# A decoder layer on eight cores: attention over the last 384 keys with a test, contiguous halves of the sequence, and pairs of tiles kept on chip

## The chip, the cores and the metric

The kernel runs on the eight cores of one Trainium2 chip as one program. The time of a run is the device time of its slowest core, in microseconds (us). Executions fall in a fast and a slow state (the kernel before took 8993 and 9005 us in its two fast runs, 9149 to 9858 in the others). The engines are PE (matmul; PEld is its weight load), DVE (VectorE), ACT (ScalarE), POOL (GpSimd) and SP, which here only issues DMAs.

## The reference, cut to what matters

```python
# x: (4, 8192, 1024) float32; 8 heads of 128; D_FF = 2816
h = x + 0.5 * swiglu(rms_norm(x), w_in1, w_out1)             # w_in: 1024 x 5632, w_out: 2816 x 1024
u = rms_norm(h)
c_b, c_c, c_x, q, k, v, g_conv, g_attn = split(u @ w_mix_in)  # 1024 x 8192
y_conv = (c_b * causal_conv3(c_c * c_x)) @ w_conv_out
# stick-breaking attention, strictly causal, z = q.k / sqrt(128):
#   a[t, s] = sigmoid(z[t, s]) * prod over s < j < t of (1 - sigmoid(z[t, j]))
y_attn = (a @ v) @ w_attn_out
h = h + (sigmoid(g_conv) * y_conv + sigmoid(g_attn) * y_attn) @ w_mix_out
h = h + 0.5 * swiglu(rms_norm(h), w_in2, w_out2)
h = h + sigmoid(rms_norm(h) @ w_ple_gate) * (p @ w_ple_proj)
return rms_norm(h)
```

The weight of a key is a product over all keys between it and the query. With factors of about one half it vanishes within some hundred keys.

## The kernel before

Two cores share a sequence. Each owns every other block of 512 tokens. In a first stage it runs the first feed-forward and the q, k, v projections, with k and v for all 8192 tokens, since attention needs them; k, q, v and the residual go to HBM. In a second stage it runs attention, and weaves everything else (`c_iter`) in, a few matmuls at a time.

```python
for i in range(NO):                              # 8 chunks of 1024 tokens, 512 of them its own
    dma(SP, xtb.dsem, xt[:], xsrc[:, :, t0:t0 + 1024], writes=[xtb])
    rmsnorm(...); ffn(..., 1024); rmsnorm(...)   # then q (512 tokens), k and v (1024 tokens)
...
top = (2 * i + 1) * 4
for gk in range(top + 3, -1, -1):                # every key tile back to token 0
    ...
# for each tile and head: scores (PE), Exp (ACT), Ln (ACT), two triangular matmuls that sum
# the logarithms over keys (PE), Exp (ACT), product (DVE), times v (PE)
...
c_advance(i)                                     # a few steps of c_iter between attention steps

def g_gate(tt, ttb, pg, pgb):                    # a sigmoid of Exp, +1 and a reciprocal
    op(ACT, lambda: nc.scalar.activation(out=tt[:], in_=pg[:], func=AF.Exp, scale=-1.0), ...)
    op(DVE, lambda: nc.vector.tensor_scalar(..., scalar1=1.0, op0=ALU.add), ...)
    op(DVE, lambda: nc.vector.reciprocal(out=tt[:], in_=tt[:]), ...)
```

At the start all weights are cast from float32 to bf16, from HBM to HBM; later they are streamed through a ring in SBUF. ACT loads its tables 18 times in the profiled run, 1283 ns each, never at these gates (L510). (Cuts are marked with dots.)

Of the kernel before, what the change touches and what calls it, by code (L numbers as in the profile page):

```python
# [9 lines left out]
BF16 = mybir.dt.bfloat16  # L10
AF = mybir.ActivationFunctionType
ALU = mybir.AluOpType

D = 1024
# [6 lines left out]
NEGBIG = -30000.0  # L21
RING = 3
SLOT_ELEMS = 4096

class Buf:
    __slots__ = ("name", "w", "r", "dsem")

    def __init__(self, name):
        self.name = name
        self.w = None  # L30
        self.r = {}
        self.dsem = None

class DSem:
    __slots__ = ("sem", "cnt")

    def __init__(self, sem):
        self.sem = sem
        self.cnt = 0

class Eng:
# [7 lines left out]
    def wait(self, ev):  # L49
        sem, val = ev  # L50
        if sem is self.sem and not self.selfwait:
            return
        if self.waited.get(sem, 0) >= val:
            return
        self.h.wait_ge(sem, val)
        self.waited[sem] = val

def _deps(reads, writes):
    deps = {}
    for b in reads:  # L60
        if b.w is not None:
            s, v = b.w
            if deps.get(s, 0) < v:
                deps[s] = v
    for b in writes:
        if b.w is not None:
            s, v = b.w
            if deps.get(s, 0) < v:
                deps[s] = v
        for s, v in b.r.items():  # L70
            if deps.get(s, 0) < v:
                deps[s] = v
    return deps

def _record(ev, reads, writes):
    s, v = ev
    for b in reads:
        if b.r.get(s, 0) < v:
            b.r[s] = v
    for b in writes:  # L80
        b.w = ev
        b.r = {}

def op(eng, fn, reads=(), writes=()):
    for s, v in _deps(reads, writes).items():
        eng.wait((s, v))
    ins = fn()
    ins.then_inc(eng.sem, 1)
    eng.cnt += 1
    ev = (eng.sem, eng.cnt)  # L90
    _record(ev, reads, writes)
    return ev

def op_group(eng, fns, reads=(), writes=()):
    for s, v in _deps(reads, writes).items():
        eng.wait((s, v))
    ins = None
    for fn in fns:
        ins = fn()
    ins.then_inc(eng.sem, 1)  # L100
    eng.cnt += 1
    ev = (eng.sem, eng.cnt)
    _record(ev, reads, writes)
    return ev

def dma(q, ds, out_ap, in_ap, reads=(), writes=(), extra=()):
    deps = _deps(reads, writes)
    for s_, v_ in extra:
        if deps.get(s_, 0) < v_:
            deps[s_] = v_  # L110
    if ds.cnt:
        if deps.get(ds.sem, 0) < ds.cnt:
            deps[ds.sem] = ds.cnt
    for s, v in deps.items():
        q.wait((s, v))
    q.h.dma_start(out=out_ap, in_=in_ap).then_inc(ds.sem, 16)
    ds.cnt += 16
    ev = (ds.sem, ds.cnt)
    _record(ev, reads, writes)
    return ev  # L120

def build(S):
    NCH = S // 512
    NO = NCH // 2
    NB = S // 128
    SO = S // 2
    nc = bass.Bass("TRN2", target_bir_lowering=False)

    def din(name, shape, dt=F32):
        return nc.dram_tensor(name, list(shape), dt, kind="ExternalInput").ap()  # L130

    xT = din("xT", [D, S])
    pT = din("pT", [PLE, SO])
    W = {
        "in1": din("w_in1", [D, 2 * DFF]),
        "out1": din("w_out1", [DFF, D]),
        "mix": din("w_mix", [D, 8 * D]),
        "co": din("w_co", [D, D]),
        "ao": din("w_ao", [D, D]),
        "mo": din("w_mo", [D, D]),  # L140
        "in2": din("w_in2", [D, 2 * DFF]),
        "out2": din("w_out2", [DFF, D]),
        "pg": din("w_pg", [D, D]),
        "pp": din("w_pp", [PLE, D]),
    }
    vecs_d = din("vecs", [128, 64])
    consts_d = din("consts", [128, 640])
    outT = nc.dram_tensor("outT", [D, SO], F32, kind="ExternalOutput").ap()

    kT_s = nc.dram_tensor("kT_s", [H, 128, S], BF16).ap()  # L150
    qT_s = nc.dram_tensor("qT_s", [H, 128, SO], BF16).ap()
    v_s = nc.dram_tensor("v_s", [128, NB, D], BF16).ap()
    h1_s = nc.dram_tensor("h1_s", [128, KC, SO], F32).ap()
    oT_s = nc.dram_tensor("oT_s", [128, H, SO], BF16).ap()

    slabs = {}

    def add_slabs(prefix, w_ap, col0, ncols, cw, nm):
        K = w_ap.shape[0]
        kc = K // 128  # L160
        ns = ncols // cw
        wb = nc.dram_tensor("wb_" + nm, [ns, 128, kc, cw], BF16).ap()
        src = w_ap.rearrange("(k p) n -> p k n", p=128)
        for j in range(ns):
            slabs[(prefix, j)] = (src[:, :, col0 + j * cw: col0 + (j + 1) * cw], wb[j], kc, cw)

    add_slabs("in1g", W["in1"], 0, DFF, 256, "in1g")
    add_slabs("in1u", W["in1"], DFF, DFF, 256, "in1u")
    add_slabs("out1", W["out1"], 0, D, 128, "out1")
    add_slabs("mix", W["mix"], 0, 8 * D, 512, "mix")  # L170
    add_slabs("co", W["co"], 0, D, 512, "co")
    add_slabs("ao", W["ao"], 0, D, 512, "ao")
    add_slabs("mo", W["mo"], 0, D, 512, "mo")
    add_slabs("in2g", W["in2"], 0, DFF, 256, "in2g")
    add_slabs("in2u", W["in2"], DFF, DFF, 256, "in2u")
    add_slabs("out2", W["out2"], 0, D, 128, "out2")
    add_slabs("pg", W["pg"], 0, D, 512, "pg")
    add_slabs("pp", W["pp"], 0, D, 1024, "pp")

    plan = []  # L180
    for i in range(NO):
        for j in range(11):
            plan += [("in1g", j), ("in1u", j)]
        plan += [("out1", dt) for dt in range(8)]
        plan += [("mix", s) for s in (6, 7, 8, 9, 10, 11)]
    for i in range(NO):
        plan += [("mix", 2), ("mix", 4), ("mix", 3), ("mix", 5)]
        plan += [("mix", 0), ("mix", 1)]
        plan += [("mix", 12), ("co", 0), ("mix", 13), ("co", 1)]
        plan += [("mix", 14), ("ao", 0), ("mix", 15), ("ao", 1)]  # L190
        plan += [("mo", 0), ("mo", 1)]
        for j in range(11):
            plan += [("in2g", j), ("in2u", j)]
        plan += [("out2", dt) for dt in range(8)]
        plan += [("pp", 0), ("pg", 0), ("pg", 1)]

    with ExitStack() as g:
# [3 lines left out]
        PE = Eng(nc.tensor, sem("s_pe"), False)  # L201
        ACT = Eng(nc.scalar, sem("s_act"), True)
        DVE = Eng(nc.vector, sem("s_dve"), True)
        POOL = Eng(nc.gpsimd, sem("s_pool"), True)
        SP = Eng(nc.sync, sem("s_sp"), False)
        engines = [PE, ACT, DVE, POOL, SP]
        dsems = []

        def new_dsem(name):
            ds = DSem(sem(name))  # L210
            dsems.append(ds)
            return ds

        def barrier():
            for e in engines:
                for f in engines:
                    if f is not e and f.cnt:
                        e.wait((f.sem, f.cnt))
                for ds in dsems:
                    if ds.cnt:  # L220
                        e.wait((ds.sem, ds.cnt))

        def sb(es, name, shape, dt, with_dsem=False):
            t = es.enter_context(nc.sbuf_tensor("sb_" + name, list(shape), dt))
            b = Buf(name)
            if with_dsem:
                b.dsem = new_dsem("d_" + name)
            return t, b

        vecs, vecs_b = sb(g, "vecs", [128, 64], F32, True)  # L230
        cst_f, cst_fb = sb(g, "cst_f", [128, 640], F32, True)
        cst_h, cst_hb = sb(g, "cst_h", [128, 640], BF16)
        epsT, eps_b = sb(g, "epsT", [128, 1], F32)
        halo, halo_b = sb(g, "halo", [128, NO, KC, 2], BF16)
        ring_t, ring_b = [], []
        for r in range(RING):
            t, b = sb(g, f"ring{r}", [128, SLOT_ELEMS], BF16, True)
            ring_t.append(t)
            ring_b.append(b)
        PS, PSb = [], []  # L240
        for r in range(8):
            t = g.enter_context(nc.psum_tensor(f"ps{r}", [128, 512], F32))
            PS.append(t)
            PSb.append(Buf(f"ps{r}"))

# [8 lines left out]
        M_incl = cst_h[:, 0:128]  # L254
        M_lt = cst_h[:, 128:256]
        ones_h = cst_h[:, 256:384]
        negm_h = cst_h[:, 384:512]
        ident_h = cst_h[:, 512:640]
        mask_f = cst_f[:, 256:384]
        negb_f = cst_f[:, 384:512]  # L260
# [630 lines left out]
```

## Time and profile before

| | before |
|---|---|
| median, 15 runs | 9439.34 us (8993.06 to 9858.19) |
| profiled run (fast) | 8997.7 us span, all cores at clock 0.922 to 0.924 |
| first 700 us | weights cast, DMA full (share 1.04) |
| 700 to 3375 us | first stage, 8192 tokens |
| 3375 to 8998 us | attention and the rest |
| PE, DVE, ACT busy | 76%, 52%, 49% |

Two things are to be read from it. The matmuls at the pace of the densest stretches (6243 us; the prediction below works it out) fill two thirds of the span, and only fewer matmuls take that away. And the last stage has three engines at 60 to 80% (PE 78%, ACT 69%, DVE 70%), waiting for each other in turn (L789 on PE 883 us and L798 on DVE 1005 us for ACT, L770 on ACT 590 us for DVE). The prediction shows the lines.

### The profile page before, as it was taken

Reading aid. Unit: us, or ns where it says so; the run is one execution under the profiler, and the core shown is the slowest. Engines: PE = TensorE matmul, PEld = TensorE weight load, DVE = VectorE, ACT = ScalarE, POOL = GpSimd, SP = SyncE. Lnnn points to the kernel's source line nnn. Section 1 sums busy time; section 2 is a strip of 40 time slices with the busy share of each in tenths; the row PEclk is TensorE's granted clock in tenths of the full one; section 3 lists DMA queues with packets and bytes.
Section 4 is the critical chain, followed back from the end, with each engine's and each line's share of the span. In section 5 each row is a group of like instructions: output and inputs, shape, how many; then the busy total and the mean of one; then the engine's idle time right before and its main releaser. Section 6 shows DMA issues by size and latency. Waiting matters only on the chain.

```text
span 8997.7 us, 105631 instructions; the slowest of 8 cores (8926.6 to 8997.7 us)
## 1 busy us (share of the span) xinstructions
PE 6873.2 (76%) x30912; PEld 2894.3 (32%) x30912; DVE 4645.7 (52%) x5709; ACT 4398.5 (49%) x8066; POOL 324.7 (4%) x353
## 2 busy tenths in 40 slices
PE   4627887888879787787887887888788778788665
PEld 1213333333334333333332333333333233333222
DVE  1002222122221224766776776677676677677676
ACT  1001111111111115768777777777777777777500
POOL 1010000000000001000000000000000000000000
PEclk8868998989989898999999999999999999999898
DMA  9993323222222223233233323322323232332222
GB/s 139 125 125 101 116 68 102 85 96 93 89 101 90 89 94 109 86 108 94 89 88 98 98 87 91 103 77 86 101 93 102 87 98 77 98 101 73 75 87 77
DMA packets 301214, 853.91 MB, mean 95 GB/s; under 512 B 62192, under 2 KB 150256, under 8 KB 270960
## 3 DMA queue, kind: packets, MB, share of 16 engines
q1 hardware_dynamic: 131488, 549.86, 18.5%
q0 software_dynamic: 169168, 297.29, 15.6%
q8 instruction: 267, 4.37, 0.2%
q14 instruction: 291, 2.38, 0.1%
HBM read 825.59 MB, written 144.18 MB: 108 GB/s over the span
## 4 chain that ended last, share of the span: by engine, by line
PE 57%; DMA 11%; ACT 11%; issue 10%; DVE 10%; another core or an unknown queue 1%; DVEq 0%; ACTq 0%; POOL 0%; SPq 0%; POOLq 0%
PE ps L307 23%; PE ps L477 18%; ACT sb_dd L796 6%; PE ps L789 5%; PE ps L792 4%; PE ps L810 4%; PE ps L753 2%; DVE sb_aa L798 2%; DVE sb_tmpC L513 2%; ACT sb_zs L770 2%; DMA sb_xt<-xT 2%; DVE sb_uA L325 2%; DMA wb_mix<-w_mix 2%; DMA wb_in1g<-w_in 1%; DMA wb_in2g<-w_in 1%
## 5 line engine op out<-in xcount | busy, mean ns | idle before, releaser
L798 DVE TENSOR_TENSOR sb_aa<-sb_zs,sb_dd 128x512 bf16<-128x512 f32 (+3 forms) x2304 | 1489.7, 657 | 1186.7 <-ACT sb_dd L796 1004.8
L307 PE MATMUL ps<-sb_uA,sb_ring 128*128 128x512 bf16 x7168 | 1618.4, 388 | 424.9 <-DVE sb_uA L325 293.0
L770 ACT ACTIVATE sb_zs<-ps 128x512 f32<-128x512 f32 (+3 forms) x2304 | 1348.8, 585 | 669.0 <-DVE sb_aa L798 590.2
L802 ACT ACTIVATE sb_sp<-sb_zs,sb_oneT 128x512 bf16<-128x512 f32 (+3 forms) x2304 | 1648.5, 716 | 1.6
L796 ACT ACTIVATE sb_dd<-ps 128x512 f32<-128x512 f32 (+3 forms) x2304 | 1355.0, 588 | 542.8 <-PE ps L792 508.6
L789 PE MATMUL ps<-sb_sp,sb_cst_h 128*128 128x512 bf16 (+2 forms) x2240 | 850.4, 380 | 886.8 <-ACT sb_dd L796 883.4
L477 PE MATMUL ps<-sb_uC,sb_ring 128*128 128x512 bf16 x5888 | 1435.5, 389 | 91.5 <-DVE sb_tmpC L640 35.7
L513 DVE RECIPROCAL sb_tmpC<-sb_tmpC 128x512 f32<-128x512 f32 x368 | 1233.9, 3353 | 39.7 <-DVE sb_tmpC L511 2.3
L307 PEld LDWEIGHTS ps<-sb_uA,sb_ring 128*128 128x128 bf16 x7168 | 708.0, 100 | 1335.3 <-issue 544.7
L810 PE MATMUL ps<-sb_aa,sb_vh 128*128 128x512 bf16 (+3 forms) x2304 | 875.6, 381 | 72.6 <-DVE sb_ost L815 61.4
L753 PE MATMUL ps<-sb_qc,sb_kh 128*128 128x512 bf16 (+3 forms) x2304 | 881.3, 383 | 43.0 <-DMA sb_kh<-kT_s 33.3
L792 PE MATMUL ps<-sb_sp,sb_cst_h 128*128 128x512 bf16 (+3 forms) x2304 | 880.8, 382 | 17.0 <-ACT sb_dd L796 17.0
L477 PEld LDWEIGHTS ps<-sb_uC,sb_ring 128*128 128x128 bf16 x5888 | 582.8, 100 | 812.4 <-issue 174.9
L348 DVE TENSOR_TENSOR sb_hidA<-sb_tmpA,ps 128x512 bf16<-128x512 f32 x352 | 241.9, 687 | 1165.0 <-PE ps L307 1147.8
L346 ACT ACTIVATE sb_tmpA<-ps 128x512 f32<-128x512 f32 x352 | 210.3, 597 | 1142.1 <-PE ps L307 1142.0
L789 PEld LDWEIGHTS ps<-sb_sp,sb_cst_h 128*128 128x128 bf16 x2240 | 218.1, 97 | 1574.1 <-issue 1464.8
L307 PE MATMUL ps<-sb_hidA,sb_ring 128*128 128x512 bf16 x2816 | 611.8, 380 | 20.9 <-DMA sb_ring<-wb_out 12.0
L314 ACT ACTIVATE sb_uA<-sb_xt 128x1024 bf16<-128x1024 f32 x128 | 135.3, 1057 | 715.6 <-DVE sb_xt L356 648.5
L307 PEld LDWEIGHTS ps<-sb_hidA,sb_ring 128*128 128x128 bf16 x2816 | 275.3, 98 | 357.3 <-issue 28.8
L356 DVE SCALAR_TENSOR_TENSOR sb_xt<-ps,sb_xt 128x512 f32<-128x512 f32 x128 | 88.5, 692 | 544.2 <-PE ps L307 544.2
L510 ACT ACTIVATE sb_tmpC<-ps 128x512 f32<-128x512 f32 x368 | 219.2, 596 | 281.0 <-PE ps L477 200.1
L307 PE MATMUL ps<-sb_ring,sb_uA 128*128 128x512 bf16 x1024 | 223.8, 381 | 161.7 <-DVE sb_stgA L410 161.7
(88 smaller groups left out, 4506.6 us busy)
## 6 DMA issues: line engine op xcount, KB each, us to landing
sb_ring<-wb_mix SPq DMA_DIRECT2D x128, 1024.0 KB, 5.5
sb_ring<-wb_out SPq DMA_DIRECT2D x128, 704.0 KB, 4.3
sb_ring<-wb_in1g SPq DMA_DIRECT2D x88, 512.0 KB, 3.8
sb_ring<-wb_in1u SPq DMA_DIRECT2D x88, 512.0 KB, 3.2
sb_ring<-wb_in2g SPq DMA_DIRECT2D x88, 512.0 KB, 3.3
sb_ring<-wb_in2u SPq DMA_DIRECT2D x88, 512.0 KB, 3.2
sb_xt<-xT SPq DMA_DIRECT2D x8, 4096.0 KB, 22.0
wb_mix<-w_mix POOLq DMA_DIRECT2D x16, 1024.0 KB, 53.5
```

The costliest lines, as they stand in the source:

```text
L307: fns.append(lambda l=l, r_=r_, t=t: nc.tensor.matmul(ps, lhsT=l, rhs=r_, start=(t == 0), stop=(t == n - 1), skip_group_check=True))
L348: op(DVE, lambda tt=tt, pu=pu, f=f, cs=cs: nc.vector.tensor_tensor(out=hid[:, f, cs], in0=tt[:], in1=pu[:], op=ALU.mult), [ttb, pub], [hidb])
L477: ins = nc.tensor.matmul(ps_ap, lhsT=l, rhs=r_, start=(t_ == 0), stop=(t_ == n_ - 1), skip_group_check=True)
L513: op(DVE, lambda: nc.vector.reciprocal(out=tt[:], in_=tt[:]), [ttb], [ttb])
L753: fz = [lambda: nc.tensor.matmul(Zp[:, c0:512], lhsT=kt[:, gk * 128:(gk + 1) * 128], rhs=qc[:, h, c0:512], start=True, stop=not dg, skip_g ...
L770: op(ACT, lambda: nc.scalar.activation(out=z[:, c0:512], in_=Zp[:, c0:512], func=AF.Exp), [Zpb], [zb_])
L789: fns.append(lambda ps_=ps_, pc0=pc0: nc.tensor.matmul(Xp[:, pc0:512], lhsT=M_lt, rhs=ps_[:, pc0:512], start=False, stop=False, skip_group ...
L792: fns.append(lambda: nc.tensor.matmul(Xp[:, c0:512], lhsT=M_incl, rhs=sp_[:, c0:512], start=(t == 0), stop=False, skip_group_check=True))
L796: op(ACT, lambda: nc.scalar.activation(out=d_[:, c0:512], in_=Xp[:, c0:512], func=AF.Exp, scale=-1.0), [Xb], [d_b])
L798: op(DVE, lambda: nc.vector.tensor_tensor(out=a_[:, c0:512], in0=z[:, c0:512], in1=d_[:, c0:512], op=ALU.mult), [zb_, d_b], [a_b])
L802: op(ACT, lambda: nc.scalar.activation(out=lsp[:, lc0:512], in_=lz[:, lc0:512], func=AF.Ln, bias=oneT[:], scale=1.0), [lzb, one_b], [lspb])
L810: op(PE, lambda: nc.tensor.matmul(Op[:, c0:512], lhsT=vt[:, gk, :], rhs=a_[:, c0:512], start=(t == 0), stop=(t == n - 1), skip_group_check ...
```

## The change

It is a rewrite. Its intent: take away about half of the matmuls (attention over 384 keys at most, the first stage on half of the tokens), keep a pair of 512-token tiles on chip through all stages, and leave PE as the only engine that matters. The core of the diff:

```diff
-            for gk in range(top + 3, -1, -1):            # all keys; Exp, Ln, triangular matmuls, Exp
+    # one slot = one head, 128 queries, up to 384 keys; issued every 12 matmuls of the other stages
+    self.act(nbt.v(0, 0, L), z, AF.Sigmoid, scale=-QS)   # 1 - sigmoid(z)
+    self.op(self.DVE, lambda: self.nc.vector.tensor_tensor_scan(       # running product, keys reversed
+        out=rv.ap, data0=nv.ap, data1=mv.ap, initial=iv, op0=ALU.mult, op1=ALU.max), ...)
+    self.tt(A.v(0, 0, L), Rt.v(0, 1, L + 1), Rt.v(0, 0, L), ALU.subtract)
...    # three transposes, a copy by ACT, three matmuls with v
+    b.op(b.POOL, lambda: b.nc.gpsimd.tensor_copy(out=f.ap, in_=end.ap), [end], [f])  # what is left
...
+    cond = nc.values_load(fli.t[0:1, 0, 0:1], ...)       # partitions with anything left
+    with nc.If(cond > 0):
+        general(...)                                     # all again, over all keys
-    g_gate(tt, ttb, pg, pgb)                             # Exp, +1, reciprocal
+    self.act(t, pg, AF.Sigmoid)
-        dma(POOL, cast_ds[n % 4], dst, src, ...)         # cast all weights, HBM to HBM, first
+    if self.first and key not in b.cast:                 # iteration 0: cast into the ring, write back
+        b.dma(b.POOL, dst, View(b.wsrc[key], [b.wres0]))
+        b.dma(b.SP, View(b.wb[key], b.wres[key]), dst)
-        xs[512:] = x[b, : S - 512]                       # every other 512 tokens
+        xs = x[bi] if hi else np.concatenate([np.zeros((HALF, D), np.float32), x[bi, :HALF]], axis=0)
...    # STAGES: in1, out1, v, qk, conv, gco, gao, mo, in2, out2, ple, for tiles A and B in turn
```

The order of the stages is fixed (in and out are the two halves of a feed-forward, gco and gao the gates and output projections of convolution and attention, mo the mix output, ple the embedding), and weights are laid out by the host so that a partition's row is one run of 8 KB or more. A core's own tokens are a contiguous half sequence; of what lies before it only 256 tokens (the halo) are needed.

## The prediction

> **What bounds the kernel now.** I read the page's slices, then the stretches of one core, then the longest pieces of the chain that ended last, then the groups of instructions.
>
> The slices and the chain's summary:
> ```profile
> span 8997.7 us, 105631 instructions; the slowest of 8 cores (8926.6 to 8997.7 us)
> PE   4627887888879787787887887888788778788665
> DVE  1002222122221224766776776677676677677676
> ACT  1001111111111115768777777777777777777500
> PEclk8868998989989898999999999999999999999898
> DMA  9993323222222223233233323322323232332222
> PE 57%; DMA 11%; ACT 11%; issue 10%; DVE 10%; another core or an unknown queue 1%; DVEq 0%; ACTq 0%; POOL 0%; SPq 0%; POOLq 0%
> ```
> There are three stages: three slices with the DMA engines full (weights are cast to bf16), twelve with PE high and the others low (first feed-forward and the q, k, v projections for all 8192 tokens), 25 with PE, DVE and ACT all at 6 to 8 (attention, with everything else woven in). The stretches give their lengths:
> ```profile
> 0.00:700.00 700.00, 309.18 (x1280) 131.27 (x1280) 78.97 (x90) 56.91 (x79) 81.89 (x93) 0.75 1.04 133
> 700.00:3375.00 2675.00, 2204.30 (x9848) 971.00 (x9849) 607.50 (x682) 440.47 (x633) 39.59 (x49) 0.91 0.28 93
> 3375.00:8998.00 5623.00, 4359.73 (x19786) 1792.02 (x19783) 3959.25 (x4937) 3901.09 (x7354) 203.18 (x211) 0.95 0.29 91
> 2720.00:2770.00 50.00, 49.90 (x231) 22.18 (x229) 10.31 (x15) 8.37 (x14) 0.00 (x0) 1.00 0.23 74
> ```
> (length, then busy us and count of PE, weight loads, DVE, ACT, POOL; clock; DMA share; GB/s.) The kernel is held by PE, but not tightly: 19,786 matmuls in 5623 us are 284 ns each, and the last row's 231 in 50 us are 216 ns. The longest pieces of the chain give the same floor:
> ```profile
> 934.14 76.15 PE ps L307 x352
> ```
> 76.15 / 352 = 216.3 ns for a matmul of 512 columns, back to back. What stretches the attention stage is visible in the groups:
> ```profile
> L798 DVE TENSOR_TENSOR sb_aa<-sb_zs,sb_dd 128x512 bf16<-128x512 f32 (+3 forms) x2304 | 1489.7, 657 | 1186.7 <-ACT sb_dd L796 1004.8
> L802 ACT ACTIVATE sb_sp<-sb_zs,sb_oneT 128x512 bf16<-128x512 f32 (+3 forms) x2304 | 1648.5, 716 | 1.6
> L789 PE MATMUL ps<-sb_sp,sb_cst_h 128*128 128x512 bf16 (+2 forms) x2240 | 850.4, 380 | 886.8 <-ACT sb_dd L796 883.4
> L513 DVE RECIPROCAL sb_tmpC<-sb_tmpC 128x512 f32<-128x512 f32 x368 | 1233.9, 3353 | 39.7 <-DVE sb_tmpC L511 2.3
> ```
> 2304 score tiles each pass PE (four matmuls), ACT (three activations) and DVE (one product) in a chain, PE idles 887 us before L789 on ACT, and sigmoids made from a 3.35 us reciprocal fill DVE.
>
> [...] the row at 2720 us has clock 1.00, and so have the other seven cores in that stretch. But it is a fast run (8999 us), and three of the four timed runs took 9549, 9809 and 9858 us[...]. [...] the 128x384 form of L798 took 548. [...]
>
> **The change part by part.** It is a rewrite with three parts.
>
> First, the attention is cut to the last three key blocks (up to 384 keys). The weight of a key is a product of (1 - sigmoid) over all later keys, and the new kernel forms this running product with a DVE scan. What is left after the window is stored for each query, and at the end a test on "is any not exactly zero" chooses whether a general, full path runs as well. I computed the reference's q and k on the host: over all queries and heads the largest logarithm left is -172.5 (first tokens, whose window is zero padding, have 256 x ln 2 = 177). float32 ends near -103, so all are zero and the general path is skipped.
>
> Second, each core owns a contiguous half sequence, not every other 512 tokens, so the k and v it needs beyond its own are those of 256 tokens. The first stage falls from 8192 to 4096 + 256 tokens.
>
> Third, tokens go in pairs of 512-token tiles through all stages, four iterations, k, q, v, hidden and residual staying on chip; sigmoid and SiLU go to ACT (no reciprocal); weights are cast on the way into the ring in iteration 0 and written back as bf16 for the other three.
>
> PE, by instructions of the built program. Before: 11,264 + 9,216 + 8,384 = 28,864 of 512 columns, 6243 us at 216.3 ns. After: 14,792 of 512 columns (1,840 for each of 8 tiles: 352 + 176 for each feed-forward, 192 q, k, v, 192 convolution, 256 gates and outputs, 64 mix output, 80 embedding; 32 for the halo's v; 40 norms): 3200 us. 594 of 256 columns for the halo, 108 ns each: 64 us. 256 attention slots, each 384 columns of scores (162 ns) and six 128-column ones, which I put at the 98 ns that a weight load takes in the trace: 0.75 us, 192 us. Sum 3456 us of PE at full clock.
>
> DVE: some 1,810 operations of 512 columns by 690 ns are 1250 us, 256 slots by a scan and a difference of about 555 ns each 285 us: 1.55 ms. ACT: 1,240 of 595 ns and 512 of 490 ns (the 128x384 row): 1.0 ms. Both lie beside PE, under half busy. The tightest place is the convolution: for 128 channels PE has 24 matmuls and two slots, 5.2 + 1.5 = 6.7 us; DVE has five operations (0.69 + 0.48 + 2 x 0.75 + 0.69 = 3.4 us) and two slots of 1.1: 5.6 us.
>
> DMA, iteration 0: 60 MB of bf16 made from 120 MB. The kernel before did it in about 690 us with full queues, and with rows of 1 or 2 KB at source; where they were 512 B (w_out, from 600 to 650 us) the cast's queue moved 5.0 MB in 50 us with all of the 16 engines' time, where they were longer (400 to 600 us) 18.1 MB in 200 us with 85% of it. [...] The new source rows are 8 KB or more. Writing 60 MB back adds about 180 us at 340 GB/s of full queues (estimate: 225 MB at 16.6% of 4000 us). So 600 to 800 us of DMA beside 870 + 50 us of PE (4,018 matmuls' worth and 64 slots): hidden, but the ring is only two groups of weights deep, so I add 60 us of stalls. Before its first matmul on weights the old kernel spent 68 us; the new one loads a 1 MB halo first: 25 us.
>
> Sum, fast state: 3456, plus 4% for stage changes, table switches and DVE in the convolution (138), plus 60, plus 25, plus 35 for the last norm, the store, the flag and the branch: about 3715 us. [...]
>
> **The rivals.** (a) Iteration 0 is bound by casting: if casting runs at the old 87 GB/s of destination and the write-back doesn't overlap, it lasts 690 + 180 + 60 = 930 us and up to 1150 with the ring's short lead: total up to 3950 fast. For: the DMA row's 9s. Against: longer rows. (b) DVE or the scan is the bound in attention: [...] a stall of 1 us in 64 pieces is 64 us. Small either way. (c) The denser PE draws the slow state in every run: 4450. For: three of four runs before were slow with PE less dense. (d) The general path runs: many times slower, over 15 ms; against it the -172.5.
>
> **Range and chances.** The time stated is a median over runs of both states. Three of four before were slow; I put 0.7 on the median being slow (4350 to 4500), the rest fast or halfway (3650 to 4050). Weighted and leaning to the slow state: 4250 us, range 3650 to 4560, which holds both. Faster by over 2%: 0.985; within: 0.005; slower: 0.01, which is the general path.
>
> **What would show it.** Right: PE at 9 in nearly all slices, 216 to 220 ns a matmul at clock 0.98 or more in a fast run; DVE and ACT under 5; the chain over 80% PE; DMA 8 or 9 only in the first quarter, then 2 or 3; the later three iterations near 880 us each. Wrong: a first quarter much longer than 1050 us with PE at 6 to 7 waiting for the ring (rival a); PE waiting for the subtraction or for a score bank in the attention stages (b); clock near 0.81 throughout (c); a second kernel's worth of matmuls at the end (d). The prediction is wrong as a whole if the later iterations are not PE-bound.

## The result and the profile after

| | before | after |
|---|---|---|
| median | 9439.34 us (15 runs) | 3639.85 us (10 runs, 3638.75 to 3949.99) |
| profiled run, span | 8997.7 us | 3640.8 us |
| PE, DVE, ACT busy | 76%, 52%, 49% | 95%, 44%, 29% |
| mean granted clock | 0.923 | 0.985 to 0.987 |
| HBM traffic of a core | 970 MB | 435 MB |

The ratio of the fast runs is 0.4045, with a 95% interval of 0.4038 to 0.4052. Ratios are the mean time of one kernel's fast runs over that of the other's fast runs of the same rounds, so not quite the quotient of the medians above. The output is right.

The slices and the chain of the changed kernel:

```profile
span 3640.8 us, 50324 instructions; the slowest of 8 cores (3634.0 to 3640.8 us)
PE   6999989999899999999989999999989999999995
DVE  4224386513631358541361238752254134854126
ACT  3111434212421244321241134422233114432113
PEclk9999999999999999999999999999999999999997
DMA  8555637866432321241322231252223231222121
PE 84%; DVE 8%; ACT 4%; issue 3%; DMA 1%; DVEq 0%; ACTq 0%; SPq 0%; POOL 0%; POOLq 0%
```

PE is at 9 nearly everywhere, its clock too, and the chain is PE's. DVE's 8s come four times, once for each iteration, where the convolution and the attention slots lie together. DMA is busier in the first quarter, but not full. The stretches are: start, iteration 0, 1, 2, 3, end (length, busy us and count of PE, weight loads, DVE, ACT, POOL; clock; DMA share; GB/s):

```profile
0.00:27.00 27.00, 0.37 (x1) 0.10 (x1) 4.30 (x13) 5.72 (x13) 4.60 (x12) 1.00 0.89 219
27.00:999.00 972.00, 931.93 (x4955) 460.85 (x4956) 419.60 (x653) 282.12 (x547) 81.64 (x180) 0.98 0.61 142
999.00:1870.00 871.00, 840.81 (x4173) 389.42 (x4171) 394.04 (x585) 258.20 (x485) 33.80 (x82) 0.99 0.27 90
1870.00:2743.00 873.00, 842.34 (x4171) 389.46 (x4170) 394.13 (x585) 258.12 (x485) 33.79 (x82) 0.99 0.27 90
2743.00:3600.00 857.00, 826.23 (x4086) 382.86 (x4086) 368.79 (x546) 241.18 (x454) 31.92 (x79) 0.98 0.24 82
3600.00:3640.80 40.80, 12.08 (x54) 5.04 (x52) 22.66 (x38) 10.55 (x17) 1.76 (x4) 0.68 0.25 106
```

Iteration 0 is 101 us longer than the next; 71 of these are the halo's matmuls (592 of 256 columns at 108 ns, 32 of 512 at 216). PE's own waits are short. The view of waits of this core, PE's rows (total us, times, longest):

```profile
PE ps L225 <- ACT sb_t L234: 31.1, 15, 4.7
PE ps L225 <- DVE sb_acchX L238: 29.5, 2, 24.8
PE ps L225 <- DVE sb_uA L241: 24.5, 20, 2.7
PE ps L504 <- ACT sb_at L234: 15.4, 21, 0.8
PE ps L225 <- DVE sb_phalo L238: 11.0, 7, 2.2
```

Of these 24.8 us are the start. No row is a DMA.

The waits seem to cost more than their own time (experiment 5 bears it out). In the trace's clock records this core has 19 stretches of 3 to 28 us, 110 us together, at half the clock; in them the matmuls of 512 columns start 427 ns apart. That is what the mean of 0.985 says. Each of the 19 begins after PE stood idle for 1.95 to 4.71 us in all within the 7 us before it. 172 matmuls start in these stretches, which makes them some 36 us longer than at the full clock (estimate: 213 ns for each 512 columns). The profiled run of the kernel before has 134 such stretches on its core 1, 1395 us together, and no other lower clock: its 0.923.

The attention slot, by its groups (count, busy us, mean ns):

```profile
L479 DVE TENSOR_TENSOR_SCAN sb_rt<-sb_nb,sb_mask 128x384 f32<-128x384 f32 x256 | 244.2, 954 | 277.7 <-ACT sb_nb L234 262.6
L491 PE MATMUL ps<-sb_ident,sb_a 128*128 128x128 bf16 x768 | 84.6, 219 | 0.0
```

The 219 ns of a 128-column matmul are not what it costs PE, as matmuls overlap. The distance from one start to the next in the trace is: 216 ns (median) for 512 columns, and 56 ns for the transposes and for the products with v. Summed from start to start, slots take 57.8 (scores) + 42.9 (transposes) + 43.2 (products) = 144 us.

### The profile page after: what moved, and what is told of

It reads as the page before. It is cut to its first block, busy times and chain, and to the rows that moved or that the text cites. A ratio compares the mean times of both kernels' runs of the same rounds, so it can differ in the third digit from the quotient of the medians.

```text
span 3640.8 us, 50324 instructions; the slowest of 8 cores (3634.0 to 3640.8 us)
## 1 busy us (share of the span) xinstructions
PE 3453.8 (95%) x17435; PEld 1627.7 (45%) x17435; DVE 1603.5 (44%) x2415; ACT 1055.9 (29%) x1997; POOL 187.5 (5%) x438
## 4 chain that ended last, share of the span: by engine, by line
PE 84%; DVE 8%; ACT 4%; issue 3%; DMA 1%; DVEq 0%; ACTq 0%; SPq 0%; POOL 0%; POOLq 0%
PE ps L225 80%; DVE sb_uB L241 1%; DVE sb_uA L241 1%; PE ps L504 1%; ACT L234 1%; PE ps L491 1%; PE ps L459 1%; DVE sb_accB L238 1%; ACT sb_t L234 1%; ACT sb_rs L234 1%; DVE sb_t L241 1%; DVE sb_accA L238 1%; DVE sb_rt L479 1%; DVE sb_t L238 0%; DMA sb_hH<-x_in 0%
## 5 line engine op out<-in xcount | busy, mean ns | idle before, releaser
L225 PE MATMUL ps<-sb_uA,sb_ring 128*128 128x512 bf16 x4864 | 1110.2, 383 | 54.7 <-DVE sb_uA L241 24.5
L225 PE MATMUL ps<-sb_uB,sb_ring 128*128 128x512 bf16 x4864 | 1104.0, 382 | 13.4 <-DVE sb_uB L241 8.5
L225 PEld LDWEIGHTS ps<-sb_uA,sb_ring 128*128 128x128 bf16 x4864 | 476.4, 99 | 626.8 <-issue 94.1
L225 PEld LDWEIGHTS ps<-sb_uB,sb_ring 128*128 128x128 bf16 x4864 | 475.1, 98 | 583.7 <-issue 46.4
L234 ACT ACTIVATE sb_t<-ps 128x512 f32<-128x512 f32 (+2 forms) x638 | 370.0, 583 | 1112.2 <-PE ps L225 1090.2
L479 DVE TENSOR_TENSOR_SCAN sb_rt<-sb_nb,sb_mask 128x384 f32<-128x384 f32 x256 | 244.2, 954 | 277.7 <-ACT sb_nb L234 262.6
L225 PE MATMUL ps<-sb_hidB,sb_ring 128*128 128x512 bf16 x1408 | 309.1, 379 | 0.0
L225 PE MATMUL ps<-sb_hidA,sb_ring 128*128 128x512 bf16 x1408 | 307.8, 379 | 0.0
L225 PEld LDWEIGHTS ps<-sb_hidB,sb_ring 128*128 128x128 bf16 x1408 | 137.8, 98 | 166.1
L238 DVE TENSOR_TENSOR sb_a<-sb_rt 128x384 bf16<-128x384 f32 x256 | 142.9, 558 | 38.6 <-DVE sb_rt L479 16.6
L234 ACT ACT_TABLE_LOAD x65 | 83.4, 1283 | 62.1 <-PE ps L225 37.5
```

Source lines behind the costliest of these rows:

```text
L225: ins = self.nc.tensor.matmul(ps.ap, lhsT=l.ap, rhs=r.ap, start=(t == 0), stop=(t == n - 1), skip_group_check=True)
L234: self.op(self.ACT, lambda: self.nc.scalar.activation(out=out.ap, in_=in_.ap, func=func, scale=scale, **kw), [in_, *extra], [out])
L238: self.op(self.DVE, lambda: self.nc.vector.tensor_tensor(out=out.ap, in0=a.ap, in1=b.ap, op=alu), [a, b], [out])
L479: self.op(self.DVE, lambda: self.nc.vector.tensor_tensor_scan(out=rv.ap, data0=nv.ap, data1=mv.ap, initial=iv, op0=ALU.mult, op1=ALU.max), ...
```

## The experiments

Twelve kernels were run, on three chips, each beside the kernel before on its own chip. These chips put cores into slow stretches in many runs (see the fourth point), so besides the times the span of the cores that no such stretch touched is given, from the profiled run; for the changed kernel it is 3634 to 3641 us.

### 1. No attention slots (e1_no_attn)

```diff
     def slot(self):
         N = len(self.items)
-        if s >= N + 3:
-            return
+        self.n += 1
+        return
+        # and fend, the flag's input, is set to 0 at the start
```

> The attention slots are not issued at all (wrong result on purpose; the flag's input is set to zero). Theory P (the changed kernel is held by PE, all else lies beside it): what goes is the slots' PE time, start to start 57.8 + 42.9 + 43.2 = 144 us in the trace, and the 36 us that PE waits in the convolution: 3460 to 3500 us. Rival D (attention is paced by its DVE work, 256 x (0.954 + 0.558) = 387 us on the path): about 3250 us.

Wrong result. Median 3765.2 us over six runs (3519.87 to 4029.16), five of them slow; undisturbed cores 3459 to 3465 us, so 177 us less. That is PE's 144 us and 33 us of waits, as theory P has it; the 387 us of DVE work were not on the path. In the window of the convolution (from the first to the last of its 16 DVE products of an iteration) 103 us became 78 us (112 and 80 in iteration 0).

### 2. Each scan twice (e2_scan_twice)

```diff
-        self.op(self.DVE, lambda: ...tensor_tensor_scan(...), [nv, mv, *extra], [rv])
+        for again in ([], [rv]):
+            self.op(self.DVE, lambda: ...tensor_tensor_scan(...), [nv, mv, *extra, *again], [rv])
```

> Each scan is issued twice (same result), 244 us more of DVE. Theory P with slack everywhere: under 15 us more, 3655 us. Theory P with DVE at its limit in the convolution alone (there 6.3 us of PE stand against 3.4 + 2 x 1.5 = 6.4 us of DVE for 128 channels, and half of the slots lie there): the 128 scans in that stage show, the others don't: +120 us, 3760 us. Rival D: all 244 us show, 3885 us.

Correct. Median 3834.34 us (five runs, one slow); undisturbed cores 3781 to 3786 us, 146 us more. So the middle theory held, 120 expected: the convolution's window went from 103 to 136 us in an iteration (112 to 144 in iteration 0), some 130 us in four, and that is most of it. In a piece of 128 channels DVE then has 3.4 + 2 x (2 x 0.954 + 0.558) = 8.3 us, and 16 pieces of it are 133. The stretch of the convolution before, and with the scan doubled:

```profile
1330.00:1430.00 100.00, 93.21 (x561) 46.51 (x570) 88.57 (x131) 38.41 (x108) 11.40 (x30) 1.00 0.22 64
```
```profile
1365.00:1495.00 130.00, 101.23 (x562) 47.74 (x560) 115.64 (x159) 38.97 (x108) 10.93 (x29) 0.95 0.15 49
```

The same 560 matmuls take 100 us at 93% of PE and 89% of DVE, then 130 us at 78% of PE with DVE still at 89%: DVE at 44% of the whole span has nothing left there.

### 3. The weights cast in every iteration (e3_cast_always)

```diff
-            if self.first and key not in b.cast:
-                b.cast.add(key)
-                b.dma(b.POOL, dst, View(b.wsrc[key], [b.wres0]))
-                b.dma(b.SP, View(b.wb[key], b.wres[key]), dst)
+            if self.first:
+                b.dma(b.POOL, dst, View(b.wsrc[key], [b.wres0]))
+                if key not in b.cast:
+                    b.cast.add(key)
+                    b.dma(b.SP, View(b.wb[key], b.wres[key]), dst)
```

> The weights are cast from float32 in all four iterations, not read back as bf16 in the last three. Theory P (casting is hidden; iteration 0 is 101 us longer than the next mainly through 71 us of halo matmuls): 3640 to 3670 us, with the DMA share of iterations 1 to 3 up from 0.27 to about 0.45. Rival A (the cast held iteration 0): 50 us or more for each of three iterations, 3790 us or more.

Correct. Median 3694.7 us (four runs). The undisturbed cores, 0, 1, 6 and 7, took 3635 to 3640 us: exactly what they took with bf16 read back. Iteration 1 with casting, on core 6:

```profile
999.00:1870.00 871.00, 837.71 (x4087) 390.05 (x4170) 395.64 (x584) 257.66 (x484) 91.34 (x192) 0.99 0.48 90
```

Its DMA share is 0.48 for 0.27, and in the same 871 us it does the same work (4170 weight loads after 4171). Casting 60 MB of bf16 from 120 MB within one iteration costs PE nothing. Rival A falls.

### 4. What the slow state is made of (the same run)

The cores of the run above were not alike:

```profile
core 0: 3639.4 us, clock 0.985
core 1: 3634.8 us, clock 0.986
core 2: 3694.0 us, clock 0.968
core 3: 3693.4 us, clock 0.970
```

One stretch of 140 us, on core 2, on core 3 and on core 0:

```profile
1020.00:1160.00 140.00, 140.00 (x535) 57.97 (x533) 27.90 (x41) 23.60 (x38) 9.57 (x18) 0.81 0.41 77
```
```profile
1020.00:1160.00 140.00, 140.00 (x535) 58.01 (x534) 28.57 (x42) 23.48 (x37) 9.54 (x18) 0.81 0.41 77
```
```profile
1020.00:1160.00 140.00, 139.32 (x637) 63.45 (x649) 32.63 (x48) 27.06 (x43) 11.66 (x22) 1.00 0.50 95
```

Cores 2 and 3 do 535 matmuls at clock 0.81 while core 0 does 637 at 1.00. The trace's clock records put cores 2 and 3 at 0.8125 from 1012 to 1174 us and again from 2784 to 2946; in 10 us steps the median distance of 512-column matmuls is 263 ns there and 216 before and after. Each such stretch costs about 162 x (1 - 216/263) = 29 us, and 3694 - 3639 = 55 us is two of them. In the profiled run of the first experiment cores 4 and 5 have stretches of 480, 160 and 160 us together, cores 6 and 7 one of some 325 at another time. So a slow run is one in which cores spend part of the time at 0.8125 of the clock, in this kernel mostly in portions of some 160 us and multiples, two neighbouring cores together. Pairs are not always independent: in f0 (point 6) cores 0 and 1 enter a stretch at 1881 us and cores 2 and 3 at 1884, and in i12 all eight cores have one of 16 us at 3602. In the long runs both pairs of a die had much of it: in this kernel's run of 4102.78 us cores 0 and 1 took 4076 and 4079, cores 2 and 3 4101 each, and the other die's four 3633 to 3635.

### 5. A reciprocal for each gate (e4_gate_recip)

```diff
         self.act(t, pg, AF.Sigmoid)
+        s = self.accx.v(0)                       # a tile that is free then
+        self.op(self.DVE, lambda: self.nc.vector.reciprocal(out=s.ap, in_=t.ap), [t, s], [s])
         return t, py
```

> One 3.35 us reciprocal on DVE, as the kernel before had it for each gate, is added to each of the 192 gates, its result unused (same output): 644 us of DVE. Worked out by stage: convolution gate: DVE 6.05 against PE 4.1 us, 64 x 1.9 = 122; attention gate 64 x 1.2 = 77; embedding gate DVE 5.4 against PE 2.2, 64 x 3.2 = 205: about +400 us, 4040 us. Rival (DVE is at 44%, so it is hidden): under 3700 us.

Correct. Median 4077.88 us (five runs, two slow); undisturbed cores 4027 to 4030 us, 392 us more, against 400 worked out by stage. PE's waits on an undisturbed core name it:

```profile
PE ps L225 <- DVE sb_t L238: 192.7, 108, 5.6
PE ps L225 <- DVE sb_hA L238: 47.3, 28, 2.6
PE ps L225 <- DVE sb_hB L238: 46.3, 26, 3.0
```

The three rows are 286 us. Much of what is left of the 392 is the clock: the waits bring PE into half-clock stretches, 312 us of them on this core for 106 in the changed kernel, and by the estimate used above their matmuls lose some 70 us more. The mean clocks of this core in the changed kernel and here show it:

```profile
core 6: 3636.1 us, clock 0.986
core 6: 4027.2 us, clock 0.962
```

An engine at 44% hid only 252 of 644 us, since work in a stage hides only behind that stage. Leaving out 192 of the old kernel's reciprocals is thus worth some 390 us here; its other 176, in the feed-forward, were not put back.

### 6. The changed kernel again, and three small edits (f0, i1, i2, i12)

> The changed kernel again, on the chip of the next three, as their base: undisturbed cores at 3634 to 3641 us. All theories: the same. Where cores are longer, a pair (0 and 1, 2 and 3, ...) is longer together, by about 27 us for each stretch of 150 us in which its 512-column matmuls are 263 ns apart and not 216 (seen in the four runs before).

Correct. Seven runs on this chip: 3642, 3664, 3668, 3669, 4073, 4103 and 4256 us; undisturbed cores 3633 to 3640, pairs with one stretch 3662 to 3667. Of the thirteen runs of the result two were slow (3902 and 3950); here three of seven, and with the three edits below 12 of 26. Whether the chip decides how often it comes, or the hour, isn't shown.

```diff
-                self.add_square(X, d - 1)                # i1: the embedding's running sum of squares
+                self.add_square(X, d - 1, True)          #     by nc.gpsimd.tensor_tensor
```

> In the embedding stage the running sum of squares (seven adds of 0.68 us for each tile and half) moves from DVE to the idle GpSimd. Theory (PE's 20 us of waits an iteration around that stage come from DVE's queue): 10 to 20 us less, 3620. Rival (they come from ACT's table switches): nothing, or a little more as GpSimd is slower.

Correct. Undisturbed cores 3630 to 3637 us: about 3 us less (median 3820.15 over six runs, three slow). An add took 1.4 to 1.5 us on GpSimd for 0.68 on DVE. PE's waits around the embedding stayed (for ACT's sb_t 30.8 us after 31.1), so they aren't made by these adds.

```diff
+                        Y.box = []                       # i2: in out2, after the sums of tile Y's next input
+                        b.hook(Y, 40, lambda Y=Y: Y.box.append(b.rstd(Y, Y.acchx, Y.rsx)))
-                                    b.norm_later(X, X.xn, 0, X.acchx, X.u, 8)
+                                    b.norm_later(X, X.xn, 0, X.acchx, X.u, 8, X.box)
```

> The inverse norms of the next iteration's inputs are computed in the second feed-forward's output stage, where ACT needs no sigmoid, not amid the embedding's sigmoids; that saves table switches of 1.28 us and a wait of ACT on PE there. Theory ACT: PE's waits of 4.7 and some 4.5 us at that place go, for three iterations: 20 to 30 us less, 3612. Rival (DVE's queue): under 5 us less.

Correct, and a miss: undisturbed cores 3648 to 3655 us, about 14 us slower (median 3803.9 over six runs, three slow). The waits moved. PE's rows:

```profile
PE ps L225 <- DVE sb_acchX L238: 50.5, 5, 25.6
...
PE ps L225 <- ACT sb_t L234: 12.6, 14, 1.5
```

The wait for ACT fell from 31.1 to 12.6 us, as meant, but PE now waits 6.7 us in each of three iterations for the sum of squares (29.5 to 50.5): the norm's matmul is issued before DVE has finished that sum. These two rows about cancel. By the two pages PE idles 9 us more in all (196 for 187) and is busy 5 us longer (3458 for 3454), with 122 us at half the clock for 110; together that is the 14 us.

> Both edits. If the waits have both causes: 30 to 45 us less, 3600 us. If one: as the better of the two.

Correct. Undisturbed cores 3641 to 3644 us (median 3647.87 over seven runs, three slow): not the 3600 of two causes, and not as good as the better edit either; 8 us better than i2, 5 worse than no edit.

### 7. An attempt at a better version (v1_better)

i1 and i2 with the delay of 40 raised to 110, and:

```diff
+        b.waits(SP, [HT.xn.ks(0, KC).res], [])          # tiles A and B are loaded after the halo
         load_x(SP, A, 0)
-        for hf in range(2):                             # last stores: two of 1 MB
+        for k0, k1 in ((0, 4), (4, 6), (6, 7), (7, 8)): # four, the last of 256 KB
```

> An attempt at a faster version: the early inverse norms, issued 110 matmuls after the sums rather than 40, since at 40 PE waited 9 us at that matmul in each iteration; the sums of squares of the embedding on GpSimd; the first tiles' input held back until the halo has landed; the last stores in smaller pieces. If the waits that the early norms removed (18 us over three iterations) stay removed without the new one: 3610 to 3620 us on undisturbed cores; less 5 for the start and 4 for the end: 3605 us. If PE's waits there come from DVE anyway: 3630.

Correct, and no gain: undisturbed cores 3650 to 3656 us, median 3665.34 over six runs, two slow. The 6.7 us waits are at the same places as in i2. The code says why: a deferred piece that belongs to a tile is flushed when the tile first enters a stage, and for tile A that comes right after it is registered, so neither 40 nor 110 is in force. Core by core against the changed kernel, the first norm matmul comes between 0.1 us later and 1.2 us earlier, and the end, from the flag's matmul on, is 1.7 to 5.2 us longer with the four stores. No version that beats the changed kernel was found; one that detaches that piece from the tile was not run.

### 8. The cut alone, in the old kernel (b1_cut_old)

```diff
-                for gk in range(top + 3, -1, -1):
+                for gk in range(top + 3, max(-1, top - 4), -1):
...    # k and v are loaded from (top - 3) * 128 on
-            G_total = sum(H * (8 * i_ + 8) + D2 for i_ in range(NO))
+            G_total = sum(H * 7 + D2 for i_ in range(NO))
```

> The kernel before with one part of the change alone: each 512-query chain of its attention stops after seven key tiles (its own four and the three before them), with the k and v loads cut to match. Same output to float32. The first 3375 us stay. Theory: what is left of the second stage (5623 us before) is paced by DVE, 2470 us of other work there with its 368 reciprocals, and 305 us of the cut products: 2775 us or somewhat more, 6150 to 6700 in all. Rival (PE paces it: 9216 + 1792 matmuls of 216 ns, 2380 us): 5760. So of the 5360 us that the change saves, the cut alone would be about half.

Correct. Median 8001.3 us (five runs); the profiled run has cores at 7760 to 7819 us. So the cut alone takes some 1200 us from the old kernel (fast runs 7820 and 7822 us, beside 9000 and 9002), not 2300 to 2850. Its second stage lasts some 4400 us, in two parts (core 4):

```profile
3375.00:5000.00 1625.00, 1033.69 (x4566) 442.22 (x4656) 913.00 (x1165) 693.04 (x1461) 138.77 (x199) 0.82 0.27 85
5000.00:7800.00 2800.00, 1704.88 (x7531) 708.78 (x7680) 1909.28 (x1915) 196.42 (x324) 9.00 (x11) 0.85 0.26 89
```

No engine is full: in the second part DVE has 68%, PE 61% and ACT 7%. Attention is done there (its last scores start at 4703 us on core 4); what is left runs alone, and norms and gates stand in its chain unhidden (on core 7 PE waits 393 us for the squares and 175 for the scaling of norms, and 244 for gates). My theory added busy time of one engine where the chain seems to have two by turns. The clock of 0.82 to 0.85 is, on core 4, nothing but half-clock stretches: 2267 us of them in the whole run, for 1395 on core 1 of the kernel before. How the 4400 us divide between norms, gates and the clock was not taken apart. A rival stands untested: the old kernel weaves in a few matmuls for each step of attention, and the cut leaves 448 steps of 2304; a weave fitted to that was not tried, so the 1200 us are the worth of the cut under the old weave.

### 9. The first input stage twice (e5_in1_twice)

```diff
     ("in1", IN_G, ("in1g", "in1u")),
+    ("in1", IN_G, ("in1g", "in1u")),
```

> The changed kernel with the first input stage of the feed-forward run twice (same output), as a measure of what a matmul costs in its dense stages: 2816 matmuls of 512 columns at 216.3 ns and 352 of 256 at 108 are 647 us: 4285 us on undisturbed cores if PE is the bound and the weights come in time. More if the ring of weights or its casting is: over 4350.

Correct. Undisturbed cores 4279 to 4287 us (4285 expected), median 4327.9 over four runs, one slow. In a dense stage a matmul costs its 216 ns and nothing else, and the weights arrive in time. By the same price the 3840 tokens that the first stage no longer sees are worth 3840/512 x 656 matmuls (528 of the feed-forward, 128 of k and v) x 0.216 = 1063 us.

### 10. The general path forced (e8_general)

```diff
-        guard = nc.If(cond > 0)
+        guard = nc.If(cond >= 0)
```

> The test at the end is forced to true, so the general path, full attention over all keys, runs after the fast one and writes the output again (same output). 20,480 matmuls of 512 columns are 4.4 ms, 4224 attention slots one after the other at an estimated 4.5 to 5 us are 19 to 21 ms: 26 to 32 ms in all, against the prediction's 'over 15 ms'.

Correct, 29140.49 us in one look. The test is thus what the speed hangs on: data with a single query that has any weight left over after the window take eight times as long, three times the old kernel's time.

## Why the prediction was right, and where it was wrong

**The mechanism held.** PE is the bound (95% busy, 84% of the chain), the later iterations take 871 and 873 us for "near 880", the general path isn't taken, and DVE and ACT lie beside PE but for the convolution, which the prediction named as the tightest place.

**The stated time was wrong**: 4250 us, where 3639.85 came, just under the low end of 3650. The step that failed is the weighing, "I put 0.7 on the median being slow", with rival (c), "The denser PE draws the slow state in every run: 4450". 11 of 13 runs of the changed kernel lie at 3639 to 3643 us, all eight cores at a mean clock of 0.985 to 0.987, and the slow two at 3902 and 3950, not 4450: on die 0 the clock was 0.89 to 0.91, not 0.81. The reason is under point 4: the low clock comes in stretches of some 160 us, mostly pair by pair. The 4450, my estimate for a whole span at the low clock, was too high as well. The slowest run seen, 4256 us, had a mean clock of 0.81 to 0.82 on its slow cores, so it was at 0.8125 nearly throughout: PE's measured 3403 us (3259 + 144, below) at 0.8125 are 4188, so some 70 us of the rest stayed visible. I put that clock on the whole span although the profile at hand showed eight dense cores at clock 1.00 (PE busy for 49.3 to 50.0 of the 50 us from 2720). Where the low clock comes, it is 0.81 indeed, with 263 ns from start to start (point 4); but in the profiled run of the changed kernel, with PE at 95%, it doesn't come: the clock records of its eight cores hold 1 and 0.5 alone. Luck has a part in this: i1 and i2 (point 6), within 14 us of the changed kernel on undisturbed cores, have medians of 3820 and 3804 on their chip, since half of their runs are slow. Why 13 of 15 runs of the kernel before were slow in the same rounds, with PE less dense, was not settled. A run of 9 ms has more room for a stretch than one of 3.6 ms, but that was not tested.

**The sum for the fast state** was 3715 us, 2% high:

| term | predicted | measured |
|---|---|---|
| matmuls of 512 and 256 columns | 3264 | 3259 (216 and 108 ns from start to start) |
| attention slots | 192 | 144 |
| stage changes, and stalls for weights | 138 + 60 | 178 |
| before the first matmul on weights | 25 | 27 |
| after the last | 35 | 29 |

(The third row is the rest of the span; 3 us are the convolution's halo.) Three terms are mis-sized. The six 128-column matmuls of a slot were put "at the 98 ns that a weight load takes": they start 56 ns apart, so weight loads overlap them, and 48 us too much came in. The "60 us of stalls" for casting in iteration 0 are not there: no row of PE's waits is a DMA, and experiment 3 casts in all four iterations at no cost. So the 178 us stand against the 138 put down for stage changes, table switches (65 loads of 1283 ns on ACT in the trace) and DVE, which was 40 too little; that the two errors nearly cancel is luck. Some 36 of the 178 are matmuls at half the clock after waits. The prediction had no term for these, though the 0.923 in the cores' view of the kernel before was made of them; it looked for a clock near 0.81 alone.

**The rivals.** (a) fell by experiment 3. (b) was half right: a scan takes 954 ns, not the about 555 of the sum, where a difference of that size took 558, and the convolution is then level between PE and DVE (93% and 89% busy, experiment 2). There the slots cost 25 us an iteration (experiment 1: 103 to 78), most of it PE's own time (32 slots of 0.56 us), and that level is why doubling the scan shows (experiment 2). (d) was real only when forced.

**Where the 5360 us went.** The parts don't add up from one-part experiments: the cut alone gives 1200 in the old kernel, under its old weave, where attention covered other work. Halving the first stage is worth 1063 us at the measured price of a matmul, and the sigmoid on ACT some 390 for 192 gates in the new schedule. The matmuls at half the clock lose some 250 us less (estimate as above: 286 before, 36 after), part of it in these shares already. The rest (tiles kept on chip, hidden norms, no casting phase of 700 us, the other reciprocals) was not taken apart.

## What to carry to other kernels

Count the matmuls and multiply by the start-to-start distance of the densest stretch in your own profile, for each width apart; with everything else hidden the span came within 7% of that sum. Judge whether another engine hides by stage, not by its share of the span: at 44% overall DVE passed on 60% of what was added to it. Read the mean granted clock too: here a mean below 1 in a fast run was made of half-clock stretches that follow PE's waits (19 in the changed kernel, 110 us, an estimated 36 lost), so a wait costs more than its own length. And weigh a slow state by the length and cost of its stretches in a trace (here 0.81 for some 160 us, 29 us each), not by its clock ratio over the whole span; how often it comes (2 of 13 runs, elsewhere 12 of 26) has to be counted.
